# Four heads of the first mixer as one rolling stream

## The chip, the core and the metric

The kernel runs on one core of one Trainium2 chip. The metric is the device time of one execution in microseconds; of several executions the median is given. The engines named below are PE (TensorE, matrix products and transposes), DVE (VectorE), ACT (ScalarE), POOL (GpSimd) and SP (SyncE, whose queue issues all the transfers).

## The reference, cut to what matters

Two layers of a block run one after the other on 1024 latent tokens and 256 context tokens. In each layer a projection feeds three mixers: a gated linear recurrence (HGRN2, the "first mixer", four heads of width 64), an mLSTM and a windowed attention; their outputs are gated, projected back and added to the input. The change is in the first mixer alone:

```python
def gla_chunked(q, k, v, logf, s0):            # chunks of L tokens
    b = jnp.cumsum(logf, axis=2)
    decay = jnp.exp(jnp.where(mask, b[:, :, :, None] - b[:, :, None, :], -jnp.inf))
    A = jnp.einsum('bnthk,bnshk,bntshk->bntsh', q, k, decay)
    o_intra = jnp.einsum('bntsh,bnshv->bnthv', A, v)
    U = jnp.einsum('bnshk,bnshv->bnhkv', k * jnp.exp(bL[:, :, None] - b), v)
    # scan over the chunks: S = exp(bL) * S + U
    o_inter = jnp.einsum('bnthk,bnhkv->bnthv', q * jnp.exp(b), s_prev)
    return (o_intra + o_inter).reshape(B, T, H, dv), s_fin
```

It runs forward and backward over the tokens; the two outputs are added, normed per head and gated.

## The kernel before, in words

**One head.** `hgrn_load` brings a head's arrays from DRAM into three tiles with five transfers: `KQ` (forward key above, query below), `QK` (the other way round) and `FG` (the forget factors of both directions). `hgrn_head` then goes through these steps, each with its line:

- `E = KQ*QK` on DVE (940), its column sums on PE into a PSUM tile `gd`, copied by ACT into the chunk matrices `AT` (944); two DVE products with `FG` (946).
- Six levels (`LEVELS`, the tokens of a chunk of 64 split in halves of 1, 2, 4, ... 32). In each, `gram` makes 40 small products (`gr`, each two PE instructions), DVE copies them under a mask into `AT` (936), and DVE multiplies the decay into `KQ`, `QK` (954) and `FG` (955). The next level's `gr` needs those products.
- The keys are transposed on PE (`ktp`) and copied by ACT into `Kt` (968), in a group of 2 and one of 8 token tiles.
- `up` products on PE; the recurrence over the 20 chunks in both directions on DVE, one small instruction for each chunk and direction (999).
- `op` products on PE: those with `AT` first, those with the states `S` after a pause; ACT copies the result into `O2` (1024). `hgrn_norm` norms two heads at a time and transposes the result (`yAp`).

**Two pairs.** `mixers` runs the heads in two pairs. `lockstep` takes the generators of a pair and always goes on with the one that is due first. Heads 0 and 2 have slots 0, 1, 2 for their three tiles, heads 1 and 3 slots 6, 7, 8 (`wt(6 * i + j, ...)`); the states later take the slot of `KQ` and `Kt` that of `FG`. So the second pair's transfers have to wait until the first pair is through. The second call of `lockstep` holds the norm of the first pair and heads 2 and 3.

**The order of work.** PE's instructions stay in the order in which the program emits them. `drive` makes that order with a clock of its own (`clk`), to which each product adds a planned time:

```python
n = max(n, 256) if rhs.dtype == F32R else 4 * (max(n, out.shape[0]) if small else n)
clk[0] += n / (4800.0 if small else 2400.0)
```

When a generator yields a number, that many microseconds of this clock are filled with products of the next projection unit (`ORDER`: `f` forget factors, `G` gates `ppGz`, `ppGo`, `e`, `c`, `d` the attention's values `ppCv`, keys `ppCk`, queries `ppCq`). `NEED` holds some units back: `e0` until the first pair is normed (`A0`), `c0`, `d0` and `G4` until all four heads are through (`o1`). Instructions of the other engines are placed by a scheduler with priorities; within the stage, copies out of a projection's PSUM tile stand above the mixer's work (`ev`). PSUM tiles come from three pools of two buffers each: `pp` (projections), `pb` (two banks: `gd`, `gr`, the larger `up`), `pm` (one bank: `ktp`, the first `up` group, `op`, `yAp`).

Of the kernel before, what the change touches and what calls it, by code (L numbers as in the profile page):

```python
# [10 lines left out]
F32 = mybir.dt.float32  # L11
# [4 lines left out]
ALU = mybir.AluOpType  # L16
# [3 lines left out]
P = 128  # L20
# [30 lines left out]
SE = 2  # L51
EV = 3500
NEED = {"p2": ("b0",), "p3": ("b1",), "e0": ("A0",), "c0": ("o1",), "d0": ("o1",), "G4": ("o1",), "e1": ("vt0",), "c1": ("s0",), "d1": ("s0",), "e2": ("vt1",), "c2": ("s1",), "d2": ("s1",), "G7": ("s1",), "W": ("c2", "d2", "e2", "G7", "gg")} | {f"o{t}": ("W",) for t in range(10)}
WAIT = {"gate": 28.0, "rot": 14.0, "qkT": 0.8, "ov": 1.4, "yB": 9.0, "load": 8.0, "gr": 4.0, "ktp": 1.5, "up": 8.0, "upc": 3.0, "yA": 9.0, "vtp": 0.5, "sc": 1.2, "sc0": 3.0, "t": 0.3, "pt": 1.2, "W": 8.0, "prep": 8.0, "st": 6.0, "y": 2.0}


def build(tc, I, out, dbg=None, upto="all"):
# [6 lines left out]
def _build(ctx, tc, nc, I, out, dbg, upto):  # L64
# [13 lines left out]
    def wt(i, shape, name, dtype=F32):  # L78
        return wk.tile(shape, dtype, tag=f"s{i}", name=name)
# [793 lines left out]
    def hgrn_f(l, h, hx):  # L873
# [14 lines left out]

        yield from proj_cm(hx, I["wcm"][l, h], ALLG, evac_f, f"Af{nm}")

    def hgrn_load(l, h):
        tok0 = TC if l == 1 else 0
        i = h % 2
        nm = f"{l}_{h}"

        KQ, QK, FG = S["A", h] = [wt(6 * i + j, [P, TA], f"{n_}{nm}") for j, n_ in enumerate(("KQ", "QK", "FG"))]
        f, w = slice(0, 64), slice(64, 128)
        q = qsd[l][h * 64:(h + 1) * 64, tok0:]
        if tok0:
            G.memset(KQ[w, 0:tok0], 0.0)  # L900
            G.memset(QK[f, 0:tok0], 0.0)
        nc.sync.dma_start(KQ[f], fsd[l][0, h, 0:64])
        nc.sync.dma_start(QK[w], fsd[l][0, h, 64:128])
        nc.sync.dma_start(KQ[w, tok0:], q)
        nc.sync.dma_start(QK[f, tok0:], q)
        nc.sync.dma_start(FG, fsd[l][1, h])

    def hgrn_head(l, h):
# [9 lines left out]
        AT = wk.tile([P, NT, LA], F32, tag=f"h{i}", name=f"AT{nm}")
        if i == 0:
            vt = wt((4, 3)[p], [P, NT, P], f"Vt{l}_{p}")  # L920
            nc.sync.dma_start(vt, vsd[l][p])
            S["V", p] = [vt]

        def gram(m, li):

# [10 lines left out]
                V.copy_predicated(v4(AT[:, y0:, :]), v4(lmask[:, li:li + 1, :].to_broadcast([P, NT - y0, LA])), src)  # L936


        E = wt(((9, 12), (9, 10))[p][i], [P, TA], f"E{nm}")
        V.tensor_tensor(E[:, tok0:], KQ[:, tok0:], QK[:, tok0:], op=ALU.mult)  # L940
        ps = pb.tile([P, 1024], F32, tag="pb", name=f"gd{nm}")
        for t in range(y0, NT):
            mm(ps[:, (t - y0) * LA:(t - y0 + 1) * LA], E[:, t * P:(t + 1) * P], ones)
        A.activation(AT[:, y0:, :], ps[:, 0:(NT - y0) * LA].rearrange("p (c t) -> p c t", t=LA), AF.Copy)
        for X, r in ((QK, f), (KQ, w)):
            V.tensor_tensor(X[r, tok0:], X[r, tok0:], FG[r, tok0:], op=ALU.mult)
        yield WAIT["gr"]
# [10 lines left out]
        dec = sm.tile([P, NCH], F32, tag="dec", name=f"dec{nm}")  # L958
        V.tensor_copy(dec, FG[:, ::LA])

        kt = wt(6 * i + 2, [P, NT, P], f"Kt{nm}")
        for t0, n in ((0, 2), (2, 8)):
            pss = [pm.tile([P, 512], F32, tag="pm", name=f"ktp{nm}_{t0}_{d}") for d in range(2)]
            for t in range(n):
                for ps, X, r in zip(pss, (KQ, QK), (f, w)):
                    tr(ps[:, t * LA:(t + 1) * LA], X[r, (t0 + t) * P:(t0 + t + 1) * P], r)
            for ps, r in zip(pss, (f, w)):
                A.activation(kt[:, t0:t0 + n, r], ps[:, 0:n * LA].rearrange("p (t c) -> p t c", c=LA), AF.Copy)
            yield WAIT["ktp"]
# [7 lines left out]
        for t0, n in ((0, 2), (2, 8)):  # L977
            ups = {}
            if not t0:
                while clk[0] < at.get("upc", 0.0):  # L980
                    yield at["upc"] - clk[0]
                at["upc"] = clk[0] + WAIT["upc"]
            if t0:
                ps = pb.tile([P, 1024], F32, tag="pb", name=f"up{nm}_{t0}")
                banks = [ps[:, 0:512], ps[:, 512:1024]]
            else:
                banks = [pm.tile([P, 512], F32, tag="pm", name=f"up{nm}_{t0}_{e}") for e in range(2)]
            for t in range(n):
# [12 lines left out]

        while f"g{h ^ 1}" not in done:
            yield 1.0
        if len(S["V", p]) == 1:
            S["V", p].append(wt((5, 10)[p], [P, NT, P], f"O2{l}_{p}"))
        Vt, O2 = S["V", p]
        for t0, n in ((0, 2), (2, 8)):
            if t0 < y0:
                continue
            ps = pm.tile([P, 512], F32, tag="pm", name=f"op{nm}_{t0}")  # L1010

            for part in range(2):
                if part and t0:
                    yield WAIT["st"]
                for t in range(t0, t0 + n):
                    for e in range(2):
                        c = 2 * t + e
                        es = slice(64 * e, 64 * e + 64)
                        o = ps[es, (t - t0) * 64:(t - t0 + 1) * 64]
                        if part:  # L1020
                            mm(o, QK[:, c * LA:(c + 1) * LA], Sx[:, c, :], False, t == t0 + n - 1)
                        else:
                            mm(o, AT[es, t, :], Vt[es, t, hs], t == t0, False)
            A.activation(O2[:, t0:t0 + n, hs], ps[:, :n * 64].rearrange("p (t v) -> p t v", v=64), AF.Copy)

    def hgrn_norm(l, p):
        y0 = NCX if l == 1 else 0
        tok0 = y0 * P
        O2 = S["V", p][1]
        n = NT - y0  # L1030
        SQ = wt((11, 3)[p], [P, NT, P], f"SQA{l}_{p}")
# [6 lines left out]
        yT = wt((11, 3)[p], [P, TA], f"yTA{l}_{p}")  # L1038
# [386 lines left out]
    for l in range(2):  # L1425
# [5 lines left out]
        def mixers():  # L1431
            yield "p0"
            yield from mlstm_gates(l)
            for h in range(HB):
                yield from flushing(mlstm_head(l, h))
            for p in range(2):
                for u in ("v", f"q{p}", f"f{2 * p}", f"f{2 * p + 1}"):
                    yield u
                if p:
                    hgrn_load(l, 2)  # L1440
                hgrn_load(l, 2 * p + 1)
                if not p:
                    yield WAIT["load"]
                pace[1] = math.inf
                ev[0] = PR + 300
                yield from flushing(lockstep([hgrn_norm(l, 0)] * p + [hgrn_head(l, 2 * p), hgrn_head(l, 2 * p + 1)], 2 + p))
            ev[0] = EV
            done.add("o1")
            pace[:] = 4.0, clk[0]
# [128 lines left out]
```

## Time and profile before

| | |
|---|---|
| median of 3 runs | 2074.26 us (2068.77 to 2077.22) |
| the profiled execution | 2070.56 us |
| its span | 2068.8 us |
| PE busy | 1825.0 us, 88% |
| DVE busy | 1288.3 us, 62% |
| mean granted clock of PE | 0.933 |

The profile shows one execution. "Busy" is the time in which an engine has an instruction under way; matrix products are pipelined, so that a busy PE need not be at its peak. The clock column of a window is the mean of the clock that PE was granted: 1.00 is 2.4 GHz, 0.50 is 1.2 GHz. A releaser is the instruction whose end let a waiting one start.

### The profile page before, as it was taken

The page shows a single profiled execution, that of the slowest core. Times are in us where ns is not written, and L with a number is a line of the kernel's source. Part 1 is how long each engine was busy: PE and PEld are TensorE (multiplying, and loading weights), DVE is VectorE, ACT ScalarE, POOL GpSimd, SP SyncE. Part 2 cuts the span into 40 slices and gives each one's busy share as a digit, 9 for nine tenths or more (in the row PEclk, how much of TensorE's full clock was granted, in tenths as well). Part 3 has the DMA queues.
Part 4 walks back from the last instruction along what each step waited for, and adds up shares of the span by engine and source line. Part 5 has one row for each costly group of instructions (what it writes and reads, how often), then busy time and mean ns, then how long its engine had stood idle before and what let it go on. Part 6 is the DMA issues. An engine that isn't in the chain of part 4 may idle for free.

```text
span 2068.8 us, 38016 instructions
## 1 busy us (share of the span) xinstructions
PE 1825.0 (88%) x14506; PEld 1567.1 (76%) x14506; DVE 1288.3 (62%) x3209; ACT 829.8 (40%) x2003; POOL 558.0 (27%) x574
## 2 busy tenths in 40 slices
PE   6979889988776989999799888999988889999798
PEld 3978778876665767878688888989867667777587
DVE  7597678667676477455465586464577754454554
ACT  5423434342011265566634334253421125454731
POOL 5342352320110211110434454234202120201512
PEclk8989999998797999999999989999998899999799
DMA  7221333441311233233743112142503112223643
GB/s 305 62 81 57 110 115 124 145 139 35 85 51 34 69 124 104 76 101 115 249 145 114 44 52 75 48 126 96 146 32 113 32 62 86 81 79 106 200 139 104
DMA packets 143287, 210.01 MB, mean 102 GB/s; under 512 B 13193, under 2 KB 77737, under 8 KB 143105
## 3 DMA queue, kind: packets, MB, share of 16 engines
q1 hardware_dynamic: 143104, 207.58, 31.3%
q8 instruction: 115, 1.88, 0.4%
q14 instruction: 68, 0.55, 0.1%
HBM read 164.83 MB, written 42.70 MB: 100 GB/s over the span
## 4 chain that ended last, share of the span: by engine, by line
PE 43%; DVE 12%; ACT 6%; issue 3%; DMA 3%; POOL 2%; SPq 0%; DVEq 0%; POOLq 0%; ACTq 0%
PE u L319 9%; PE ppGz L319 5%; PE ppB L319 4%; PE ppCk L319 4%; PE sc L319 3%; PE ppCq L319 3%; PE ppCv L319 2%; PE ppAf L319 2%; PE ppGo L319 2%; DVE S L999 2%; ACT S L1170 1%; PE tw L324 1%; ACT S L1172 1%; DVE dj L199 1%; PE ov L319 1%
## 5 line engine op out<-in xcount | busy, mean ns | idle before, releaser
L319 PE MATMUL ppB<-whB,hh 128*128 128x288 f32 (+3 forms) x640 | 197.7, 309 | 25.8 <-ACT Vx L610 20.0
L319 PE MATMUL ppB<-whB,hl 128*128 128x288 f32 (+3 forms) x640 | 192.2, 300 | 1.0 <-DVE hl L293 1.0
L319 PE MATMUL ppB<-wlB,hh 128*128 128x288 f32 (+3 forms) x640 | 192.3, 301 | 0.0
L319 PE MATMUL u<-ow,yh 128*128 128x512 f32 (+1 forms) x684 | 182.9, 362 | 2.3 <-ACT u L1404 1.8
L319 PE MATMUL ppGz<-hh,whGz 128*128 128x512 f32 (+1 forms) x320 | 134.5, 420 | 25.2 <-DVE cv L1080 14.8
L199 DVE CUSTOM_DVE_ANT_0 dj<-wm,crows 128x256 bf16<-128x256 f32 x256 | 130.9, 511 | 27.7 <-DMA wm<-in_w_mod 24.3
L319 PEld LDWEIGHTS ppB<-whB,hh 128*128 128x128 f32 x640 | 124.5, 195 | 29.1 <-ACT Vx L610 22.5
L319 PEld LDWEIGHTS u<-ow,yh 128*128 128x128 f32 x684 | 124.1, 191 | 24.1 <-ACT u L1404 2.6
L319 PE MATMUL ppGz<-hl,whGz 128*128 128x512 f32 (+1 forms) x320 | 125.8, 393 | 0.0
L319 PE MATMUL ppGz<-hh,wlGz 128*128 128x512 f32 (+1 forms) x320 | 125.4, 392 | 0.0
L319 PEld LDWEIGHTS ppB<-whB,hl 128*128 128x128 f32 x640 | 124.2, 194 | 1.3 <-DVE hl L293 1.3
L319 PEld LDWEIGHTS ppB<-wlB,hh 128*128 128x128 f32 x640 | 124.6, 195 | 0.1
L319 PE MATMUL u<-ow,yl 128*128 128x512 f32 (+1 forms) x324 | 114.7, 372 | 4.8 <-POOL yl L1315 4.8
L319 PEld LDWEIGHTS ppGz<-hh,whGz 128*128 128x128 f32 x320 | 65.3, 204 | 37.1 <-issue 15.4
L329 POOL TENSOR_TENSOR wlGz<-wrGz,whGz 128x512 fp32r<-128x512 f32 x32 | 45.0, 1408 | 174.4 <-PE ppGz L319 45.7
L999 DVE SCALAR_TENSOR_TENSOR S<-S,dec,up 64x64 f32<-64x64 f32 x288 | 80.5, 280 | 9.3
L319 PEld LDWEIGHTS gr<-QK,KQ 64*64 64x64 f32 x1728 | 57.9, 140 | 37.5 <-issue 30.1
L319 PE MATMUL gr<-QK,KQ 64*64 64x32 f32 x1728 | 61.9, 225 | 27.3 <-DVE QK L954 27.2
L1170 ACT ACTIVATE S<-S,nmx 128x544 f32<-128x544 f32 (+1 forms) x96 | 75.0, 783 | 22.9 <-DVE nmx L1168 22.4
L319 PE MATMUL ppAf<-hh,whAf 128*128 128x512 f32 (+1 forms) x192 | 77.6, 404 | 4.8 <-DVE fe L884 4.8
L1283 POOL TENSOR_TENSOR ow<-wro,ow 128x256 fp32r<-128x256 f32 (+1 forms) x44 | 43.4, 1017 | 123.0 <-ACT ow L1282 122.8
L1168 DVE CUSTOM_DVE_ANT_0 S<-sc,bias 128x544 f32<-128x544 f32 (+1 forms) x96 | 70.9, 768 | 8.1 <-PE sc L319 8.0
(464 smaller groups left out, 5394.2 us busy)
## 6 DMA issues: line engine op xcount, KB each, us to landing
wm<-in_w_mod SPq DMA_DIRECT2D x64, 256.0 KB
bias<-in_rpb SPq DMA_DIRECT2D x48, 320.0 KB
bias<-in_rpb SPq DMA_DIRECT2D x48, 272.0 KB
ygr<-gTd SPq DMA_DIRECT2D x36, 256.0 KB
wm<-in_w_first SPq DMA_DIRECT2D x16, 512.0 KB
wrGz<-in_wcm SPq DMA_DIRECT2D x32, 256.0 KB
gTd<-gz SPq DMA_DIRECT2D x32, 256.0 KB
wro<-in_w_out SPq DMA_DIRECT2D x32, 256.0 KB
```

The lines of the kernel that those rows point to most:

```text
L199: V.tensor_tensor_reduce(out=junk, in0=w, in1=r, scale=1.0, scalar=0.0, op0=ALU.mult, op1=ALU.add, accum_out=dst[:, i:i + 1])
L319: return PE.matmul(out, lhsT=lhsT, rhs=rhs, start=start, stop=stop)
L324: return PE.transpose(out, x, ident[r, r])
L329: (eng or G).tensor_tensor(wl, raw, wh.bitcast(F32), op=ALU.subtract)
L999: V.scalar_tensor_tensor(Sx[r, nx, :], Sx[r, c, :], dec[r, c:c + 1], ups[c][r], op0=ALU.mult, op1=ALU.add)
L1168: V.tensor_tensor_reduce(out=S2, in0=ps[i][:, 512 - nk:512 + TC], in1=bias[i][:, :nk + TC] if nk else zero.to_broadcast([P, TC]), scale=-1 ...
L1170: A.activation(S2, S2, AF.Exp, scale=-1.0, bias=nmx[:, o], accum_out=den[:, o])
L1172: A.activation(S2, S2, AF.Copy, scale=den[:, o])
L1283: G.tensor_tensor(w, raw[:, c:c + n], h.bitcast(F32), op=ALU.subtract)
```

## The change

The four heads become one stream: `lockstep([head 0, head 1, head 2, norm of 0 and 1, head 3], 3)` with three places. Head 2 has tiles of its own (slots 9, 12, 10) and is loaded at the start, once its projections are done. It makes `E` and the two `FG` products, and then waits for `x0`, the mark that head 0 is through. Head 3 takes the place of head 1 and its slots; it loads once `x1` is set. `AT`, `gd` and the transfer of `Vt` come after the `FG` products, behind a planned pause `gd` of 4 us. The key transposes go direction by direction, each in a `pm` tile of its own taken in turn; the first `up` group takes a `pb` tile, as the second does. `E`, `Vt`, `O2` and the tiles of the norm change slots.

```diff
+    HSL = ((0, 1, 2), (6, 7, 8), (9, 12, 10), (6, 7, 8))
...
+        if p:
+            while not all(u in done for u in (f"q{p}", f"f{h}")) or i and f"x{h - 2}" not in done:
+                yield 1.0
+            hgrn_load(l, h)
         KQ, QK, FG = S["A", h]
...
+        if p:
+            yield WAIT["load"]
+        E = wt((5, 11, 11, 0)[h], [P, TA], f"E{nm}")
         V.tensor_tensor(E[:, tok0:], KQ[:, tok0:], QK[:, tok0:], op=ALU.mult)
+        for X, r in ((QK, f), (KQ, w)):
+            V.tensor_tensor(X[r, tok0:], X[r, tok0:], FG[r, tok0:], op=ALU.mult)
+        yield WAIT["gd"]
+        while p and f"x{h - 2}" not in done:
+            yield 1.0
+        AT = wk.tile([P, NT, LA], F32, tag=f"h{i}", name=f"AT{nm}")
         ps = pb.tile([P, 1024], F32, tag="pb", name=f"gd{nm}")
...
-        for X, r in ((QK, f), (KQ, w)):
-            V.tensor_tensor(X[r, tok0:], X[r, tok0:], FG[r, tok0:], op=ALU.mult)
-        yield WAIT["gr"]
+        if i == 0:
+            vt = wt((4, 11)[p], [P, NT, P], f"Vt{l}_{p}")
+            nc.sync.dma_start(vt, vsd[l][p])
+            S["V", p] = [vt]
+        yield 1.0
...
         for t0, n in ((0, 2), (2, 8)):
-            pss = [pm.tile([P, 512], F32, tag="pm", name=f"ktp{nm}_{t0}_{d}") for d in range(2)]
-            for t in range(n):
-                for ps, X, r in zip(pss, (KQ, QK), (f, w)):
+            for X, r in ((KQ, f), (QK, w)):
+                ps = pm.tile([P, 512], F32, tag="pm", name=f"ktp{nm}_{t0}_{r.start}")
+                for t in range(n):
                     tr(ps[:, t * LA:(t + 1) * LA], X[r, (t0 + t) * P:(t0 + t + 1) * P], r)
-            for ps, r in zip(pss, (f, w)):
                 A.activation(kt[:, t0:t0 + n, r], ps[:, 0:n * LA].rearrange("p (t c) -> p t c", c=LA), AF.Copy)
             yield WAIT["ktp"]
...
-            if t0:
-                ps = pb.tile([P, 1024], F32, tag="pb", name=f"up{nm}_{t0}")
-                banks = [ps[:, 0:512], ps[:, 512:1024]]
-            else:
-                banks = [pm.tile([P, 512], F32, tag="pm", name=f"up{nm}_{t0}_{e}") for e in range(2)]
+            ps = pb.tile([P, 1024], F32, tag="pb", name=f"up{nm}_{t0}")
+            banks = [ps[:, 0:512], ps[:, 512:1024]]
...
-        while f"g{h ^ 1}" not in done:
-            yield 1.0
...
+        done.add(f"x{h}")
...
-            for p in range(2):
-                for u in ("v", f"q{p}", f"f{2 * p}", f"f{2 * p + 1}"):
-                    yield u
-                if p:
-                    hgrn_load(l, 2)
-                hgrn_load(l, 2 * p + 1)
-                if not p:
-                    yield WAIT["load"]
-                pace[1] = math.inf
-                ev[0] = PR + 300
-                yield from flushing(lockstep([hgrn_norm(l, 0)] * p + [hgrn_head(l, 2 * p), hgrn_head(l, 2 * p + 1)], 2 + p))
+            for u in ("v", "q0", "f0", "f1"):
+                yield u
+            hgrn_load(l, 1)
+            yield WAIT["load"]
+            pace[1] = math.inf
+            ev[0] = PR + 300
+            yield from flushing(lockstep([hgrn_head(l, 0), hgrn_head(l, 1), hgrn_head(l, 2), hgrn_norm(l, 0), hgrn_head(l, 3)], 3))
```

## Rows read from the trace of the kernel before

**Rows 1.** The page, part 1: busy time, share of the span, count, by engine.

```profile
PE 1825.0 (88%) x14506; PEld 1567.1 (76%) x14506; DVE 1288.3 (62%) x3209; ACT 829.8 (40%) x2003; POOL 558.0 (27%) x574
```

**Rows 2.** Windows, first layer: length, busy PE, PEld, DVE, ACT, POOL (count), clock, DMA share, GB/s.

```profile
459.22:497.70 38.48, 32.59 (x1027) 28.11 (x1026) 35.83 (x61) 4.18 (x8) 2.88 (x2) 0.91 0.14 49
497.70:551.99 54.29, 44.35 (x401) 36.05 (x400) 27.12 (x87) 11.02 (x21) 4.32 (x8) 0.81 0.21 63
551.99:573.64 21.65, 13.46 (x56) 12.12 (x55) 11.82 (x8) 2.64 (x4) 11.11 (x5) 0.61 0.42 95
573.64:616.03 42.39, 32.90 (x1035) 28.28 (x1035) 39.81 (x73) 4.18 (x8) 6.49 (x4) 0.92 0.19 62
616.03:680.19 64.16, 45.03 (x402) 36.71 (x401) 31.52 (x118) 10.69 (x22) 3.99 (x7) 0.81 0.09 27
```

**Rows 3.** The same for the second pair of heads in the second layer.

```profile
1575.20:1593.88 18.68, 12.33 (x60) 10.80 (x55) 9.82 (x8) 1.79 (x3) 6.37 (x8) 0.63 0.42 101
1593.88:1634.28 40.40, 33.01 (x859) 28.06 (x858) 36.24 (x58) 5.26 (x9) 9.33 (x6) 0.92 0.15 48
1634.28:1685.20 50.92, 42.53 (x351) 32.73 (x350) 26.01 (x90) 12.12 (x24) 5.72 (x8) 0.87 0.08 27
```

**Rows 4.** Waits from 440 to 700 us: who waited for whom, total, times, longest.

```profile
PE ppGz L319 <- DVE cv L1080: 9.1, 1, 9.1
PE op L319 <- ACT O L1024: 5.9, 2, 5.5
PE ktp L324 <- DVE S L999: 5.2, 2, 3.0
PE ktp L324 <- ACT Kt L968: 4.6, 4, 1.6
```

**Rows 5.** Waits from 1480 to 1700 us.

```profile
PE ppGz L319 <- DVE cv L1080: 5.8, 1, 5.8
PE ktp L324 <- ACT Kt L968: 2.6, 2, 1.3
```

**Rows 6.** Timeline of the SP queue and of VectorE in the first layer's gap.

```profile
552.04 0.44 SPq L902 DMA_DIRECT2D KQ<-fsd  x1
563.18 1.48 DVE L940 TENSOR_TENSOR E<-KQ,QK 128x1280 f32<-128x1280 f32 x1
```

**Rows 7.** Windows of the first pair's level stretch: tile gr alone, then line 954 alone.

```profile
459.22:497.70 38.48, 17.31 (x960) 16.21 (x960) 13.53 (x24) 0.91 0.14 49
459.22:497.70 38.48, 18.35 (x23) 0.91 0.14 49
```

**Rows 8.** Windows of tile ppAf alone, from gd on, first and second layer.

```profile
437.90:703.15 265.25, 0.00 (x0) 0.00 (x0) 0.68 (x1) 1.73 (x3) 0.85 0.21 64
1473.70:1702.03 228.33, 0.00 (x0) 0.00 (x0) 0.68 (x1) 1.71 (x3) 0.88 0.23 71
```

**Rows 9.** Windows of tile gd alone: first and second pair, first layer; second pair, second layer.

```profile
450.30:455.00 4.70, 4.57 (x40) 4.45 (x40) 0.73 (x2) 1.00 0.18 57
551.99:573.64 21.65, 9.06 (x40) 8.68 (x40) 1.41 (x2) 0.61 0.42 95
1575.20:1593.88 18.68, 7.30 (x32) 6.98 (x32) 1.19 (x2) 0.63 0.42 101
```

**Rows 10.** Timeline of PE: key transposes of one head, first layer.

```profile
500.38 0.22 PE L324 MATMUL ktp<-ident,KQ 64*128 64x64 f32 x1
500.38 0.22 PE L324 MATMUL ktp<-ident,QK 64*128 64x64 f32 x1
500.75 0.22 PE L324 MATMUL ktp<-ident,KQ 64*128 64x64 f32 x1
```

**Rows 11.** Windows of VectorE alone, between gd and the first level copies, first layer.

```profile
452.00:460.60 8.60, 0.69 (x1) 1.00 0.43 115
```

**Rows 12.** Windows of line 999 alone, a stretch with nothing between its instructions.

```profile
656.50:666.60 10.10, 8.95 (x32) 1.00 0.07 25
```

**Rows 13.** Windows of tile ppGz alone, after head 3's end, second layer.

```profile
1685.20:1702.03 16.83, 9.94 (x42) 7.82 (x42) 2.07 (x3) 2.58 (x5) 1.00 0.36 125
```

More of the change, by code (lines that the diff above doesn't have):

```diff
@@ L53 @@
 NEED = {"p2": ("b0",), "p3": ("b1",), "e0": ("A0",), "c0": ("o1",), "d0": ("o1",), "G4": ("o1",), "e1": ("vt0",), "c1": ("s0",), "d1": ("s0",), "e2": ("vt1",), "c2": ("s1",), "d2": ("s1",), "G7": ("s1",), "W": ("c2", "d2", "e2", "G7", "gg")} | {f"o{t}": ("W",) for t in range(10)}
-WAIT = {"gate": 28.0, "rot": 14.0, "qkT": 0.8, "ov": 1.4, "yB": 9.0, "load": 8.0, "gr": 4.0, "ktp": 1.5, "up": 8.0, "upc": 3.0, "yA": 9.0, "vtp": 0.5, "sc": 1.2, "sc0": 3.0, "t": 0.3, "pt": 1.2, "W": 8.0, "prep": 8.0, "st": 6.0, "y": 2.0}
+WAIT = {"gate": 28.0, "rot": 14.0, "qkT": 0.8, "ov": 1.4, "yB": 9.0, "load": 8.0, "gr": 4.0, "ktp": 1.5, "up": 8.0, "upc": 3.0, "yA": 9.0, "vtp": 0.5, "sc": 1.2, "sc0": 3.0, "t": 0.3, "pt": 1.2, "W": 8.0, "prep": 8.0, "gd": 4.0, "st": 6.0, "y": 2.0}
 def build(tc, I, out, dbg=None, upto="all"):
@@ L889, in hgrn_f @@
         yield from proj_cm(hx, I["wcm"][l, h], ALLG, evac_f, f"Af{nm}")
+    HSL = ((0, 1, 2), (6, 7, 8), (9, 12, 10), (6, 7, 8))
     def hgrn_load(l, h):
         tok0 = TC if l == 1 else 0
-        i = h % 2
         nm = f"{l}_{h}"
-        KQ, QK, FG = S["A", h] = [wt(6 * i + j, [P, TA], f"{n_}{nm}") for j, n_ in enumerate(("KQ", "QK", "FG"))]
+        KQ, QK, FG = S["A", h] = [wt(HSL[h][j], [P, TA], f"{n_}{nm}") for j, n_ in enumerate(("KQ", "QK", "FG"))]
         f, w = slice(0, 64), slice(64, 128)
@@ L915, in hgrn_head @@
         hs = slice(64 * i, 64 * i + 64)
+        if p:
+            while not all(u in done for u in (f"q{p}", f"f{h}")) or i and f"x{h - 2}" not in done:
+                yield 1.0
+            hgrn_load(l, h)
         KQ, QK, FG = S["A", h]
[L918 to L922, printed above, removed]
         def gram(m, li):
@@ L936, in gram @@
                 V.copy_predicated(v4(AT[:, y0:, :]), v4(lmask[:, li:li + 1, :].to_broadcast([P, NT - y0, LA])), src)
-        E = wt(((9, 12), (9, 10))[p][i], [P, TA], f"E{nm}")
+        if p:
+            yield WAIT["load"]
+        E = wt((5, 11, 11, 0)[h], [P, TA], f"E{nm}")
         V.tensor_tensor(E[:, tok0:], KQ[:, tok0:], QK[:, tok0:], op=ALU.mult)
+        for X, r in ((QK, f), (KQ, w)):
[4 more added lines that the diff above has]
+        AT = wk.tile([P, NT, LA], F32, tag=f"h{i}", name=f"AT{nm}")
         ps = pb.tile([P, 1024], F32, tag="pb", name=f"gd{nm}")
@@ L959, in hgrn_head @@
         V.tensor_copy(dec, FG[:, ::LA])
-        kt = wt(6 * i + 2, [P, NT, P], f"Kt{nm}")
+        kt = wt(HSL[h][2], [P, NT, P], f"Kt{nm}")
         for t0, n in ((0, 2), (2, 8)):
-            pss = [pm.tile([P, 512], F32, tag="pm", name=f"ktp{nm}_{t0}_{d}") for d in range(2)]
-            for t in range(n):
-                for ps, X, r in zip(pss, (KQ, QK), (f, w)):
+            for X, r in ((KQ, f), (QK, w)):
+                ps = pm.tile([P, 512], F32, tag="pm", name=f"ktp{nm}_{t0}_{r.start}")
+                for t in range(n):
                     tr(ps[:, t * LA:(t + 1) * LA], X[r, (t0 + t) * P:(t0 + t + 1) * P], r)
-            for ps, r in zip(pss, (f, w)):
                 A.activation(kt[:, t0:t0 + n, r], ps[:, 0:n * LA].rearrange("p (t c) -> p t c", c=LA), AF.Copy)
@@ L970, in hgrn_head @@
         A.activation(QK[w, tok0:], KQ[w, tok0:], AF.Copy)
-        Sx = wt(6 * i, [P, NCH, LA], f"S{nm}")
+        Sx = wt(HSL[h][0], [P, NCH, LA], f"S{nm}")
         G.memset(Sx[f, 0, :], 0.0)
@@ L1000, in hgrn_head @@
             yield WAIT["up"] if t0 else WAIT["upc"]
-        while f"g{h ^ 1}" not in done:
-            yield 1.0
         if len(S["V", p]) == 1:
-            S["V", p].append(wt((5, 10)[p], [P, NT, P], f"O2{l}_{p}"))
+            S["V", p].append(wt((5, 1)[p], [P, NT, P], f"O2{l}_{p}"))
         Vt, O2 = S["V", p]
@@ L1024, in hgrn_head @@
             A.activation(O2[:, t0:t0 + n, hs], ps[:, :n * 64].rearrange("p (t v) -> p t v", v=64), AF.Copy)
+        done.add(f"x{h}")
     def hgrn_norm(l, p):
+        while any(f"x{2 * p + i}" not in done for i in range(2)):
+            yield 1.0
         y0 = NCX if l == 1 else 0
@@ L1030, in hgrn_norm @@
         n = NT - y0
-        SQ = wt((11, 3)[p], [P, NT, P], f"SQA{l}_{p}")
+        SQ = wt(3, [P, NT, P], f"SQA{l}_{p}")
         G.tensor_tensor(SQ[:, y0:], O2[:, y0:], O2[:, y0:], op=ALU.mult)
@@ L1037, in hgrn_norm @@
         V.tensor_tensor(O2v, O2v, r[:, :, None].to_broadcast([P, 2 * n, 64]), op=ALU.mult)
-        yT = wt((11, 3)[p], [P, TA], f"yTA{l}_{p}")
+        yT = wt(3, [P, TA], f"yTA{l}_{p}")
         yield WAIT["yA"]
```

## The prediction

> **What bounds the kernel now.** I read the page's first part, then windows over the stage of the first mixer in both layers, then the waits in it, then the timelines of its gap. The page shows PE busy 88% of the span [rows 1]: outside the stage only PE work itself could be shortened, and the change shortens none. So the question is how much PE idle time, or time at a low clock, the stage holds and what ends it.
>
> The windows cut the stage by what PE does: levels of the first pair, its transposes, `up` and `op`, then the gap from the last `op` to the first `gr` of the second pair, then the second pair [rows 2, 3]. In the first layer PE is idle 38.48 - 32.59 = 5.9, 9.9, 8.2, 9.5 and 19.1 us in the five stretches. In the second layer the gap, levels and rest of the second pair hold 6.4, 7.4 and 8.4 us. The gaps also have the lowest clock, 0.61 and 0.63. In the levels DVE is the fuller engine: 35.83 of 38.48 us.
>
> The waits name what PE stands for outside the levels [rows 4, 5]: key transposes for ACT's copies and for the recurrence (5.2 + 4.6 and 2.6 us; both hold `pm` tiles), a gate product for an attention value copy on DVE (9.1 and 5.8 us, DVE being in the recurrence), `op` for ACT (5.9 us). In the gap SP issues head 3's first transfer only at 552.04, when the first pair is done, and `E` of that head begins at 563.18 [rows 6]; `gd`, next in PE's fixed order, stands behind it with everything that follows.
>
> One head alone: a level has a gram of 17.31/12 = 1.44 us on PE and 35.83/12 = 2.99 us on DVE [rows 2, 7], of which the copies are 13.53/12 = 1.13 and line 954 is 18.35/23 x 2 = 1.60. These follow one another: 4.4 us. The planner sets 4 us of other products between two grams of one head, so 1.44 + 4.0 = 5.4 us: with one head in its levels PE waits for nothing. With two, 38.48/6 = 6.4 us for both, and DVE decides.
>
> **The change part by part.** Reference is the profiled execution, 2070.56 us (span 2068.8); the median of the runs, 2074.26, is 3.7 above it.
>
> *Head 2 loaded early.* It polls for `q1` and `f2`; no forget product runs in either layer from `gd` on [rows 8], so the load goes out at the stage's start, five transfers where the DMA share of the following levels is 0.14 [rows 2]. That moves its loads ahead of the level stretch in SP's queue, and `Vt` behind `gd`; the count of transfers stays. At `x0` head 2 needs only `gd` and its grams, beside projection products. The gap's idle goes: 8.2 + 6.4 = 14.6 us. Its low clock goes in part: `gd` costs 9.06 us there for 40 instructions, 4.57 us in the first pair of the first layer, and 7.30 us for 32 in the second layer, which at the first pair's price is 3.66 [rows 9]: 4.5 + 3.6 us. Together 22.7; I take 20, because head 3's `gd` still comes in the middle of things. Lower end 8, the first layer's idle alone.
>
> *Head 3 loaded after `x1`.* On the planner's clock it comes 8 (load) + 4 (`gd`) + 1 us after head 1. From transfer to `E` took 563.18 - 552.04 = 11.1 us, so PE, with 13 us of other products in front, should not wait. Head 2 has 13/5.4 = 2.4 levels done by then; some three levels run as a pair, the rest of head 3's alone at PE's pace. The second pair's levels hold 9.5 + 7.4 = 16.9 us of PE idle; I take back half, 8 (0 to 17).
>
> *Key transposes and first `up` group.* A `pm` tile each in turn, and `up` in `pb`: the waits for `pm`, 5.2 + 4.6 + 2.6 = 12.4 us, lose their cause except for ACT's copies themselves. I take 6 (0 to 12).
>
> *Order of the transposes.* Today those on `KQ` and `QK` start together, and seven of each take 500.75 - 500.38 = 0.37 us for six steps, 0.062 a step [rows 10]. If only the pairing gives that, eight and two steps for each direction in turn add 10 x 0.062 = 0.62 us for a head, 5 us for eight heads; if not, nothing. I take 2, as ACT now copies the one while PE transposes the other. The Trainium skill (TensorEngine Tiling (Array Packing), Tiling Modes, Key Properties) says that different tiles of the array run weight loads and products in parallel, which speaks against this edit. By that rule the 5 us stand whole and the sum below is 3 us worse; the row agrees that the two halves overlap, and does not show one half alone.
>
> *`E` and the `FG` products of head 2 among the levels of the first pair.* Three DVE operations; `E` takes 1.48 us [rows 6], the other two have as many columns: 4.5 us, and 4/5 of it, 3.6, in the second layer with 1024 columns instead of 1280. The DVE has room just before, 0.69 us busy of 8.60 [rows 11], but the planner places them after the first grams. Loss 6 us (0 to 8). Behind them wait the level copies, and the next gram for those.
>
> *Recurrence of head 2 within head 3's levels.* A new wait. The 30 instructions after the second `up` group take 10.10/32 = 0.316 us each [rows 12], 9.5 us. If DVE does them in one run, a level of head 3 stands behind it, and PE's next gram, with all projection products after it, waits 9.5 - 4 = 5.5 us a layer. Loss 11 us (0 to 30, see the slow rival).
>
> *Recurrences apart instead of together.* The copies that held PE up, 9.1 + 5.9 + 5.8 = 20.8 us [rows 4, 5], stood behind two heads' recurrences at once, 60 instructions or 19 us; now behind one at a time. I take back half, 10 (0 to 21).
>
> *Projection products.* Head 3's 13 us of pauses and the single levels ask for more of them inside the stage: the 13 less what head 2's grams fill (2.4 x 1.44), about 9.5 us, a little more at the pair's end. The second layer has only 9.94 us of gate products left after head 3 [rows 13]; units behind `o1` can't come earlier. Once they are used up PE runs on the heads alone. Loss 3 us (0 to 5).
>
> *Nothing:* the marks and the lockstep of three cost no instruction. `O2` of the second pair lies in slot 1, which the attention's first transposed values take next; PE's `yAp` transposes stand right before these in its order, so the slot is free by then. If that cover went, the copy would wait for the one transpose group ahead of it, under a microsecond. `E` in 5, 11 and 0 and `Vt` in 11 take slots whose last readers are PE instructions well ahead.
>
> **Sum:** 20 + 8 + 6 + 10 = 44 us back, 2 + 6 + 11 + 3 = 22 us lost: 22 us. 2070.56 - 22 = 2048.6; with 3.7 us for the median, **2052 us**. It assumes that idle taken from PE in the stage shortens the whole: the gate products not used there come after it, among attention work whose PE share is that of the kernel or higher.
>
> **The rivals.**
> *No change.* The end of the stage is set by head 3, whose load still waits for head 1, and which has 13 us of pauses more than the pair had. Head 2's head start then only moves projection products forward, and the low clock, the level idle and the copies stay as they are. What is left is the gap's idle, 14.6, less 6, 11 and 3: -5, so 2070.56 + 5 + 3.7 = 2079 us; without the new wait 2069. For it speaks that head 3's chain of levels is as long as before; against it, that single levels are PE's, not DVE's.
>
> *Slower: the recurrence holds `pb`.* One mechanism: head 2's second `up` group keeps one of the two `pb` tiles until its recurrence ends, and head 3's grams, one `pb` tile each, run into it; PE stands still in its fixed order. In the first layer the recurrences were drawn out by other DVE work (the rest of the second pair, 64 us, has only 31.52 us of DVE [rows 2]), so a tile can be held far longer than 9.5 us. Without this term the sum is 33 us gained; it decides from 33/2 = 16.5 us a layer, and is visibly slower from 22. At 25 us a layer the time is 2070.56 - 33 + 50 + 3.7 = 2091 us. Against it: with one head in levels a single `pb` tile is enough, because the next gram waits for DVE anyway.
>
> *Much faster.* All waits named go and nothing new comes: 22.7 + 16.9 + 12.4 + 20.8 = 72.8, less 8 and 5: 60 us, so 2014 us.
>
> *The early load isn't early*, because SP's queue stands at that time behind a transfer that waits. Then the gap moves but stays: 20 us less gained, 2072 us. It belongs with no change.
>
> **How the numbers follow.** A run of this kernel can be told from no change at about 0.5%, 10.4 us: below 2063.9 is faster, above 2084.6 slower. The forecast, with its own range of 2040 to 2066 (none of the new wait, or some half of the gains with unknown ends gone), has 0.55; much faster 0.11; no change with the late load 0.20; the slow rival 0.14. A little of the no-change case falls on either side: faster 0.66, same 0.20, slower 0.14. The range is 2024 to 2088: it leaves out most of the much faster case and the worse part of the slow one.
>
> **What would show it.** Right: between head 0's last `op` and head 2's first `gr` some 4 us instead of 21.65 and 18.68 to the second pair's; `E` of head 2 at the first pair's start; the clock there above 0.9; single grams with 18 projection instructions between them; waits of `ktp` nearly gone. Wrong: a wait of `gr` for line 999 longer than 6 us, or of `gd` of head 3 for its `E`; the first pair's levels longer than 44 us; a second layer in which PE has no projection product left before head 3 is through. The prediction is wrong above all if these new waits, or a later end of head 3, cost as much as the gaps held.

## The result, and the profile after

The changed kernel takes 2034.53 us in the median (2030.47 to 2039.9) against 2073.58 for the kernel before on the same chip: a ratio of 0.9817, 95% interval 0.9801 to 0.9833. That is 39 us less where 22 were forecast: direction right and inside the stated range of 2024 to 2088, but 1.8 times the size, and below the 2040 to 2066 that the forecast gave its own main case. The profiled execution spans 2031.0 us, 37.8 less than before.

The page, part 1, of the changed kernel, answers to [rows 1]. PE's instructions are the same in number, and take 18.1 us less.

```profile
PE 1806.9 (89%) x14506; PEld 1552.8 (76%) x14506; DVE 1298.8 (64%) x3209; ACT 829.2 (41%) x2003; POOL 559.1 (28%) x574
```

Windows over the whole stage, from the last forget product to the first attention query product, in both layers; first the kernel before, then the changed one (columns as in [rows 2]).

```profile
437.84:717.63 279.79, 220.33 (x3182) 184.13 (x3182) 177.59 (x417) 51.77 (x107) 46.15 (x37) 0.85 0.21 64
1473.63:1714.96 241.33, 206.74 (x2666) 168.19 (x2666) 152.47 (x329) 52.61 (x101) 46.63 (x46) 0.89 0.22 68
```

```profile
431.32:690.16 258.84, 213.12 (x3182) 180.08 (x3182) 178.06 (x388) 50.51 (x103) 45.86 (x39) 0.88 0.21 65
1449.47:1676.09 226.62, 198.36 (x2667) 161.56 (x2667) 154.79 (x333) 52.89 (x103) 47.71 (x43) 0.93 0.22 69
```

PE does the same instructions in both, give or take one. The two stages together went from 521.1 to 485.5 us, and these 35.6 us are nearly all of the gain. PE idle (length less busy) fell from 94.1 to 74.0 us, by 20. PE busy fell from 427.1 to 411.5, by 15.6: the same products at a higher granted clock. A second profile of the changed kernel (e9, below) has 77.0 us of idle and 408.1 us of PE busy in its two stages.

Windows of the changed kernel's first layer, in the order of [rows 2]: levels of the first pair; its transposes, `up` and `op`; the rest, in two parts, to the last `op` of head 3. The last row is the second layer's second stretch.

```profile
460.79:500.57 39.78, 33.56 (x1029) 29.51 (x1030) 39.20 (x63) 4.48 (x9) 1.50 (x1) 0.87 0.08 26
500.57:541.49 40.92, 37.83 (x415) 31.74 (x418) 26.50 (x87) 11.23 (x22) 4.03 (x7) 1.00 0.15 50
541.49:599.02 57.53, 42.53 (x831) 36.35 (x831) 43.33 (x63) 6.97 (x12) 16.91 (x9) 0.76 0.25 73
599.02:662.66 63.64, 56.26 (x696) 46.79 (x695) 39.29 (x123) 12.29 (x25) 8.31 (x10) 0.95 0.10 34
...
1514.87:1554.50 39.63, 39.09 (x425) 31.33 (x425) 26.32 (x86) 11.65 (x22) 9.32 (x12) 1.00 0.18 60
```

The second stretch took 54.29 us and now takes 40.92, at a clock of 1.00 instead of 0.81. The gap is gone as a stretch. The third row is left at a low clock, 0.76.

PE's waits in the changed kernel, stage of the first layer, then of the second.

```profile
PE gr L319 <- DVE QK L965: 12.2, 10, 2.9
PE ppGz L319 <- DVE fe L884: 9.1, 1, 9.1
PE yAp L324 <- DVE O L1045: 8.9, 1, 8.9
PE ppGz L319 <- DVE cv L1088: 6.5, 1, 6.5
...
PE ktp L324 <- ACT Kt L978: 1.2, 3, 0.7
...
PE op L319 <- ACT O L1029: 0.4, 1, 0.4
...
PE gr L319 <- DVE S L1006: 0.2, 1, 0.2
```

```profile
PE gr L319 <- DVE QK L965: 14.6, 8, 6.2
PE ppGz L319 <- DVE fe L884: 4.2, 2, 3.2
PE op L319 <- ACT Kt L978: 3.1, 1, 3.1
```

Against [rows 4, 5] the waits of `ktp` for the recurrence are gone, that of `op` for ACT is 0.4, that of the gate product for `cv` 6.5 once. The wait charged with 11 us, `gr` for the recurrence (now line 1006), is 0.2. New are 9.1 us for `fe` (3.1 before) and 8.9 us of the norm's transposes, `yAp`, for the norm's product.

### The profile page after: what moved, and what is told of

Same layout as the page of the kernel before. It is cut to its first block, busy times and chain, and to the rows that moved or that the text cites. A ratio compares the mean times of both kernels' runs of the same rounds, so it can differ in the third digit from the quotient of the medians.

```text
span 2031.0 us, 37975 instructions
## 1 busy us (share of the span) xinstructions
PE 1806.9 (89%) x14506; PEld 1552.8 (76%) x14506; DVE 1298.8 (64%) x3209; ACT 829.2 (41%) x2003; POOL 559.1 (28%) x574
## 4 chain that ended last, share of the span: by engine, by line
PE 54%; DVE 22%; ACT 7%; issue 5%; DMA 4%; POOL 4%; SPq 0%; DVEq 0%; POOLq 0%; ACTq 0%
PE u L319 9%; PE ppB L319 7%; PE ppGz L319 6%; PE ppCk L319 4%; DVE dj L199 4%; PE ppCq L319 3%; PE sc L319 3%; PE ppAf L319 3%; PE ppCv L319 2%; PE ppAq L319 2%; PE ppGo L319 2%; PE ppAv L319 2%; DVE AT L936 2%; DVE S L1006 2%; ACT S L1178 2%
## 5 line engine op out<-in xcount | busy, mean ns | idle before, releaser
L199 DVE CUSTOM_DVE_ANT_0 dj<-wm,crows 128x256 bf16<-128x256 f32 x256 | 135.9, 531 | 20.7 <-DMA wm<-in_w_mod 17.3
```

Of the source, the lines that this page charges most:

```text
L199: V.tensor_tensor_reduce(out=junk, in0=w, in1=r, scale=1.0, scalar=0.0, op0=ALU.mult, op1=ALU.add, accum_out=dst[:, i:i + 1])
```

## The experiments

The edits are shown against the kernel before, or against the changed one where that is said.

### The buffers alone

**e1_buffers_alone**: the kernel before, with key transposes direction by direction and the first `up` group in `pb`. **e6_up_in_pb_alone**: the second hunk alone.

```diff
-            pss = [pm.tile([P, 512], F32, tag="pm", name=f"ktp{nm}_{t0}_{d}") for d in range(2)]
-            for t in range(n):
-                for ps, X, r in zip(pss, (KQ, QK), (f, w)):
+            for X, r in ((KQ, f), (QK, w)):
+                ps = pm.tile([P, 512], F32, tag="pm", name=f"ktp{nm}_{t0}_{r.start}")
+                for t in range(n):
...
-            for ps, r in zip(pss, (f, w)):
...
-            if t0:
-                ps = pb.tile([P, 1024], F32, tag="pb", name=f"up{nm}_{t0}")
-                banks = [ps[:, 0:512], ps[:, 512:1024]]
-            else:
-                banks = [pm.tile([P, 512], F32, tag="pm", name=f"up{nm}_{t0}_{e}") for e in range(2)]
+            ps = pb.tile([P, 1024], F32, tag="pb", name=f"up{nm}_{t0}")
+            banks = [ps[:, 0:512], ps[:, 512:1024]]
```

> The kernel before with the buffers alone changed: key transposes direction by direction in a pm tile each, first up group in pb; the two pairs stay. Theory A (the head start of head 2 and the filled gap are the bulk, the buffers some 6 us as the prediction has it): ratio to before 0.995 to 0.999, and the first layer's stretch from the first pair's last gr to its last op shrinks from 54.3 us by at most 5. Theory B (the buffers are worth a third or more of the 39 us): ratio 0.990 or less, and that stretch near 41 us, as in the changed kernel.

> The kernel before with only the first up group moved from two pm tiles to pb. If the buffers' gain comes from the pm tiles that the first up group holds until the recurrence has read them (second head's key transposes waiting 5.2 us in the first layer, and what stands behind them), this has most of it: ratio 0.988 to 0.994. If the order of the key transposes is what gains (each direction's copy beside the other's transposes), this has little: 0.996 to 1.000.

Measured: e1 2052.28 us, 0.9898 (0.9857 to 0.9938); e6 2053.52 us, 0.9898 (0.9863 to 0.9932). So this edit is worth some 1.0%, 21 us (the intervals allow 13 to 30), where the prediction took 6; and as far as these intervals tell, all of it comes from `up` leaving `pm`, since e6 has no other edit. The order of the transposes costs and gives nothing that can be measured here. In e1 the stretch from the first pair's key transposes to its last `op` was 49.63 us where the kernel before had 54.29 and the changed kernel 40.92: in the full change something more acts on it. That rest is mostly clock, since idle is 4.9 us in e1 and 3.1 in the changed kernel, PE busy 44.7 and 37.8.

Windows of e6, the four stretches after the first pair's levels, as in [rows 2], and its waits of `ktp` in the first layer.

```profile
497.50:546.00 48.50, 41.53 (x401) 33.78 (x400) 27.13 (x87) 11.02 (x21) 4.31 (x8) 0.89 0.23 70
546.00:568.20 22.20, 13.90 (x57) 12.43 (x55) 11.82 (x8) 2.63 (x4) 11.13 (x5) 0.62 0.41 94
568.20:610.20 42.00, 34.52 (x1031) 29.81 (x1031) 39.97 (x71) 4.18 (x8) 6.49 (x4) 0.84 0.20 62
610.20:668.60 58.40, 43.90 (x406) 35.82 (x404) 31.12 (x121) 10.70 (x22) 3.98 (x7) 0.85 0.10 30
```

```profile
PE ktp L324 <- ACT Kt L968: 4.6, 4, 1.6
```

The wait for the recurrence (5.2 us) is gone, that for ACT's copies stays at 4.6. The first pair's last stretch lost 5.8 us with the same 401 PE instructions: 3.0 of idle (9.94 to 6.97) and 2.8 of PE busy (44.35 to 41.53), at a clock of 0.89 instead of 0.81. The second pair, from its first gram to its last `op`, lost 6.2 (106.55 to 100.40). Half of what the first stretch gained stands in no row of waits. This split is not the same in every execution: in e1 the stretch lost 5.0 us of idle and nothing of PE busy (44.71 us, clock 0.83).

**e2_old_buffers_pair1**: the changed kernel, heads 0 and 1 with the old buffers.

```diff
+            if p == 0:
+                pss = [pm.tile([P, 512], F32, tag="pm", name=f"ktp{nm}_{t0}_{d}") for d in range(2)]
...
+            else:
+                for X, r in ((KQ, f), (QK, w)):
...
+            if t0 or p:
                 ps = pb.tile([P, 1024], F32, tag="pb", name=f"up{nm}_{t0}")
```

> The changed kernel with heads 0 and 1 alone back on the old buffers (both directions' key transposes at once, first up group in two pm tiles); heads 2 and 3 keep the new ones, which they need when they overlap. Theory A: ratio to before 0.982 to 0.985, at most 6 us slower than the changed kernel. Theory B: 12 to 16 us slower than the changed kernel, ratio 0.987 to 0.990, with the stretch from the first pair's last gr to its last op in the first layer back at some 54 us.

Measured: 2042.76 us, 0.9836 (0.9805 to 0.9866); the changed kernel has 0.9817. Inside the rolling stream the buffers of the first pair are worth a few us at most, and the intervals overlap. The first layer's stretch from transposes to last `op` took 45.28 us, 4.4 more than in the changed kernel, not the 54 of theory B. Old buffers for heads 2 and 3 in the stream weren't tried: two `pm` tiles held there would stand in PE's fixed order in front of other heads' transposes.

### The gap without an early load

**e3_pause_only**: the kernel before, where the second pair too yields for the load's planned time. Nothing is loaded earlier; the planner puts projection products in front of `gd`.

```diff
                 hgrn_load(l, 2 * p + 1)
-                if not p:
-                    yield WAIT["load"]
+                yield WAIT["load"]
```

> The kernel before, with the planned pause of 8 us after the loads also ahead of the second pair; nothing is loaded earlier. If the gap costs because PE's order has nothing to do in it (theory C: filling is all, the head start gains nothing of its own), this gains what the gap held, 14 to 20 us: ratio 0.990 to 0.993. If the head start is what gains (theory A), the pause only moves products into the gap while the second pair starts no earlier, and the ratio is 0.995 to 1.000.

Measured: 2044.27 us, 0.984 (0.9816 to 0.9865): 1.6% from one line, 33 us, more than the theories expected. Windows of e3, the gap in both layers, which answer to the third row of [rows 2] and the first of [rows 3]:

```profile
552.71:574.54 21.83, 19.77 (x136) 17.47 (x133) 14.07 (x10) 4.38 (x7) 15.14 (x8) 0.92 0.56 131
1562.40:1578.66 16.26, 16.26 (x88) 13.54 (x87) 11.86 (x10) 3.49 (x7) 9.02 (x9) 1.00 0.52 128
```

The gap is as long as before in the first layer (21.83 against 21.65), but PE fills it: 136 instructions instead of 56, idle 2.1 us instead of 8.2, clock 0.92 instead of 0.61. In the second layer idle goes from 6.4 to nothing and the clock from 0.63 to 1.00. The transfers are no earlier: `E` of the second pair begins at 558.81 (557.21 before), and what PE still waits for it is the 2.1 us. The gaps' 12.5 us of idle are not the whole. Over both stages idle fell from 94.1 to 74.0 and PE busy from 427.1 to 415.5; the gate product's waits for `cv` (9.1 and 5.8 us before) are gone as well, while `op` now waits 12.5 us for ACT instead of 5.9.

**e5_pause_and_buffers**, and again in five rounds as **e10_pause_buffers_5_rounds**: e3 and e1 together, without rolling and without an early load. **e9_changed_again**: the changed kernel, five rounds on that same chip.

The edits are those two, shown above.

> The kernel before with the pause ahead of the second pair and the new buffers, no early load and no rolling: the two parts that gained 1.6% and 1.0% alone. Theory C (filling the gap and the buffers are the whole gain; loading head 2 ahead and rolling add nothing): ratio 0.974 to 0.983, as fast as the changed kernel or faster. Theory A' (the head start of head 2 still gives a part): the two overlap, ratio 0.984 to 0.988, slower than the changed kernel by 5 us or more.

> Pause and buffers on the kernel before, no early load and no rolling, now beside the changed kernel in five rounds. Theory C (rolling and the early load add nothing): no slower than the changed kernel, ratio 0.974 to 0.982. Theory A' (they add a part): slower, 0.984 or more.

> The changed kernel itself, beside the next three on the same chip: ratio 0.980 to 0.984 by every theory.

Measured: e5 2025.37 us, 0.9768 (0.9726 to 0.981); e10 2028.56 us, 0.9788 (0.9765 to 0.981); e9 2036.7 us, 0.9842 (0.9816 to 0.9868). On one chip the pause and the buffers beat the changed kernel by 8 us, with intervals that don't meet. The gains add up nearly: 1.6% and 1.0% apart, 2.1 to 2.3% together. So the rolling stream and the early load, together and as built here, are no gain over the pause and the buffers; they cost some 0.4 to 0.5%. Early load and rolling were not run apart from each other.

Windows over the two stages of e5, which has e10's code (for e10 see below):

```profile
436.43:687.52 251.09, 209.94 (x3183) 176.70 (x3182) 172.14 (x395) 50.49 (x103) 43.90 (x37) 0.90 0.23 70
1447.43:1664.83 217.40, 196.11 (x2668) 159.23 (x2666) 151.54 (x329) 52.23 (x101) 46.87 (x46) 0.95 0.25 75
```

Idle in the two stages is 62.4 us in e5 and 60.8 in e10, against 74.0 and 77.0 in the two profiles of the changed kernel: the stream's loss is idle. PE busy tells less: 406.1 in e5 and 415.2 in e10, 9.1 us apart with the same code and work.

The stream does win one wait. The largest that pause and buffers leave, from the waits of e10 in the first layer, is 0.4 us in the changed kernel:

```profile
PE op L319 <- ACT O L1020: 13.2, 2, 12.8
```

### What the rolling stream costs

Timelines of the changed kernel, first layer: VectorE, then ScalarE and PE, ahead of the first pair.

```profile
432.83 2.57 DVE L944 TENSOR_TENSOR QK<-QK,FG 64x1280 f32<-64x1280 f32 x1
435.41 1.49 DVE L944 TENSOR_TENSOR KQ<-KQ,FG 64x1280 f32<-64x1280 f32 x1
...
437.67 1.48 DVE L942 TENSOR_TENSOR E<-KQ,QK 128x1280 f32<-128x1280 f32 x1
...
439.42 1.47 DVE L944 TENSOR_TENSOR QK<-QK,FG 64x1280 f32<-64x1280 f32 x1
440.90 1.49 DVE L944 TENSOR_TENSOR KQ<-KQ,FG 64x1280 f32<-64x1280 f32 x1
...
442.50 0.68 DVE L884 SCALAR_TENSOR_TENSOR fe<-fe,ppAf 128x512 f32<-128x512 f32 x1
```

```profile
439.46 0.28 ACT L838 ACTIVATE nu<-H 128x96 f32<-128x96 f32 x1 [5.96 <-DVE H L836]
...
443.24 0.80 PE L319 MATMUL ppGz<-hh,whGz 128*128 128x512 f32 x1 [9.08 <-DVE fe L884]
```

The program now has the `FG` products of heads 0 and 1 before `gd`. On DVE all four run between the end of the last forget product (431.32) and the last forget gate's `fe`, which frees the tile that a gate product needs. In the kernel before, head 0's pair ran at 426.03, ahead of that end (437.84), and head 1's at 443.68, behind `fe`. Part of the delay goes by way of ACT, which makes the input of `fe` and stands 5.96 us behind a DVE result of the mLSTM. PE waits 9.1 us there; e10 and e3, with the program's old order, wait 3.8 and 4.8. The prediction saw that the `FG` products move among the first pair's levels for head 2, and costed nothing for heads 0 and 1. No run moved them alone, so this cause is read from the order, not shown by an edit.

Windows of the changed kernel around the wait of `yAp`:

```profile
549.00:562.00 13.00, 4.10 (x72) 3.19 (x65) 12.28 (x11) 1.26 (x2) 7.25 (x4) 0.83 0.22 66
562.00:575.00 13.00, 13.00 (x142) 11.18 (x141) 3.11 (x6) 2.28 (x4) 0.00 (x0) 0.52 0.13 52
```

The norm of the first pair is planned between heads, and its product (560.17) comes on DVE behind `E`, both `FG` products of head 3 and a level. PE's fixed order holds `yAp` in front, so PE does 4.1 us of work in 13. Then it has work without a pause for 13 us, at a clock of 0.52: the wait is paid a second time.

**e7_norm_later**: the changed kernel, with that order moved.

```diff
-        yield WAIT["yA"]
+        yield 20.0 if p == 0 else WAIT["yA"]
```

> The changed kernel with a planned pause of 20 us instead of 9 between the norm of the first pair and its transposes. In the changed kernel PE stands 8.9 us in the first layer at these transposes, waiting for the normed output, and 6.2 us in the second just ahead of them. If these are pauses planned too short, the ratio is 0.973 to 0.979, 5 to 15 us faster than the changed kernel; if the wait only moves on (the grams behind then wait for DVE), 0.980 to 0.984.

Measured: 2030.74 us, 0.9789 (0.9757 to 0.9821). The wait of `yAp` for the norm's product is gone, the first layer's stage is 254.85 us instead of 258.84; but `gr` now waits 16.8 us there instead of 12.2. By ratio it is better by 0.3%, inside the intervals.

**e4_E_after_x0**: the changed kernel, with `E` and the `FG` products of head 2 held until head 0 is through (head 3 waits for head 1 in any case, before its load).

```diff
+        while p and f"x{h - 2}" not in done:
+            yield 1.0
         E = wt((5, 11, 11, 0)[h], [P, TA], f"E{nm}")
```

> The changed kernel with head 2 still loaded early, but its E and FG products only after head 0 is through. The prediction charged 6 us for these three DVE operations among the first pair's levels. If that holds, the first pair's levels shorten by some 4 us in the first and 3 in the second layer, and what is lost at head 2's start (4.5 us of DVE and the 4 us pause ahead of its gd, with other products in it) is less: ratio 0.977 to 0.982, that is 0 to 8 us faster than the changed kernel. If their place is worth it, 3 to 10 us slower: 0.983 to 0.987.

Windows of e4, levels of the first pair, first and second layer; in the changed kernel 39.78 and 38.74.

```profile
466.44:503.91 37.47, 29.66 (x1019) 26.35 (x1018) 36.95 (x58) 4.33 (x8) 1.50 (x1) 0.91 0.06 21
1475.58:1511.36 35.78, 30.88 (x830) 25.75 (x829) 34.14 (x58) 3.50 (x6) 2.80 (x2) 0.90 0.11 34
```

The levels are 2.3 and 3.0 us shorter: 5.3, against the 6 of the prediction. The whole, 2035.86 us and 0.9801 (0.9777 to 0.9824), is not told apart from the changed kernel. Its stage is 254.88 us in the first layer, 4.0 shorter, and 231.77 in the second, 5.2 longer; what was lost there was not followed up.

**e8_head3_in_head0_slots**: the changed kernel, with head 3 loaded after head 0 instead of head 1, into head 0's tiles, and the norm of heads 0 and 1 taken into the stream after head 3. **e12_roll_and_norm**: e8 with the edit of e7.

```diff
-    HSL = ((0, 1, 2), (6, 7, 8), (9, 12, 10), (6, 7, 8))
+    HSL = ((0, 1, 2), (6, 7, 8), (9, 12, 10), (0, 1, 2))
...
-            while not all(u in done for u in (f"q{p}", f"f{h}")) or i and f"x{h - 2}" not in done:
+            while not all(u in done for u in (f"q{p}", f"f{h}")) or i and "x0" not in done:
...
-        E = wt((5, 11, 11, 0)[h], [P, TA], f"E{nm}")
+        E = wt((5, 11, 11, 8)[h], [P, TA], f"E{nm}")
...
-            S["V", p].append(wt((5, 1)[p], [P, NT, P], f"O2{l}_{p}"))
+            S["V", p].append(wt((5, 10)[p], [P, NT, P], f"O2{l}_{p}"))
...
-            yield from flushing(lockstep([hgrn_head(l, 0), hgrn_head(l, 1), hgrn_head(l, 2), hgrn_norm(l, 0), hgrn_head(l, 3)], 3))
+            yield from flushing(lockstep([hgrn_head(l, 0), hgrn_head(l, 1), hgrn_head(l, 2), hgrn_head(l, 3), hgrn_norm(l, 0)], 3))
```

> The changed kernel with head 3 in the slots of head 0 and taken into the stream when head 0 is through, so that its load starts 5 us earlier and its pauses run before head 1 ends; the norm comes after it. If head 3's late start sets the end of the stage (the rival 'no change' of the prediction, which held that its 13 us of pauses eat the head start), this gains 4 to 10 us over the changed kernel: ratio 0.975 to 0.979. If the stage is filled with projection products anyway, the same as the changed kernel: 0.980 to 0.983.

> The changed kernel with both of the edits that gained over it one by one: head 3 in the slots of head 0, and the norm's transposes 20 planned us after the norm. If the two gains (some 9 and 5 us) have different causes they add: ratio 0.972 to 0.976. If both only fill the same gap: 0.976 to 0.979.

Measured: e8 2027.68 us, 0.977 (0.9743 to 0.9797); e12 2027.53 us, 0.9789 (0.9766 to 0.9812). Both are some 0.5% faster than the changed kernel, by intervals that don't meet: e8 against its first measurement (0.9817, on another chip), e12 against e9 on the same chip. That fits a cost of head 3's late load, as the rival of no change had it though not in its size; but e8 also moves the norm, and the two were not run apart. The edit of e7 adds nothing on top. Built this way the stream is level with pause and buffers: 2027.53 us against 2028.56 on one chip.

### The best version

**e11_pause_buffers_norm**: e10 with the one line of e7.

> The same with the norm's transposes of the first pair 20 instead of 9 planned us after the norm. In the pairs the norm's transposes stand between two planned grams, with a wait of ACT of some 2.5 us in the first layer: if such waits are all that is left of short pauses, 0 to 5 us faster than without, ratio 0.973 to 0.979; if the delay takes e0 out of reach, slower, 0.980.

Windows over the whole stage, e10, then e11:

```profile
441.55:697.49 255.94, 216.31 (x3183) 181.95 (x3182) 170.77 (x392) 50.04 (x101) 44.08 (x37) 0.87 0.22 67
1454.89:1674.91 220.02, 198.89 (x2666) 162.02 (x2666) 151.55 (x329) 52.37 (x101) 47.57 (x46) 0.94 0.24 74
```

```profile
438.98:687.17 248.19, 207.92 (x3183) 174.90 (x3182) 171.96 (x395) 50.45 (x103) 43.65 (x37) 0.91 0.23 70
1446.54:1663.06 216.52, 195.98 (x2667) 159.96 (x2666) 152.46 (x329) 52.10 (x101) 47.94 (x46) 0.94 0.25 75
```

Measured: 2020.06 us, 0.9754 (0.9727 to 0.9781), 52 us less than the kernel before and 17 less than the changed one on that chip; its interval overlaps e10's a little, and e5's by more. Against e10's profile the first layer's stage is 7.8 us shorter: PE busy fell by 8.4, at a clock of 0.91 instead of 0.87, and idle rose from 39.6 to 40.3. That step is clock, and it is not shown to come from the edit: e5, with e10's code, has a stage of 251.09 us at 0.90, and its profiled execution (2019.24 us) is as fast as e11's (2020.06). Whether the line gains anything over e10 stays open.

## Why the prediction was right in sign and short in size

**What bounds it** held: the gain lies in the two stages, 35.6 of 37.8 us. What failed is how it was counted. The prediction priced the low clock in the gap alone, 4.5 and 3.6 us; elsewhere a wait counted by its length. PE busy at equal work gave 15.6 and 19.0 us in the two profiles of the changed kernel, 11.9 and 21.0 in those of pause and buffers (e10, e5), and 23.2 in e11. Idle fell by 20.1 us, near the net of 22 that was forecast for idle and the gap's clock, but that is luck: as the next paragraphs show, the terms were off in both directions, and two waits stood in none of them.

**Recurrence of head 2 within head 3's levels, 11 us charged: 0.2 measured.** The step that failed most. The changed kernel's windows of tile `gr` alone, from where head 2's recurrence begins (611.2):

```profile
610.00:625.00 15.00, 1.37 (x80) 1.29 (x80) 0.89 (x2) 0.91 0.16 54
625.00:640.00 15.00, 0.00 (x0) 0.00 (x0) 0.00 (x0) 0.86 0.03 10
```

A level has 80 of these instructions (960/12 in [rows 7]): one gram of head 3 was left, and it waited 0.2 us. The lead of 2.4 levels was nearly right: three grams of head 2 ran before head 3's first. What the prediction left out is the time between head 2's last gram and its recurrence, 15.8 us here (595.40 to 611.21), filled with its transposes and first `up` products; head 3 made two of its last three grams in it. DVE in the same stretch:

```profile
611.21 8.39 DVE L1006 SCALAR_TENSOR_TENSOR S<-S,dec,up 64x64 f32<-64x64 f32 x27
619.53 0.89 DVE L936 COPY_PREDICATED AT<-lmask,gr 128x320 f32<-128x320 uint8 x2
```

The copy of head 3's last gram (done at 614.57) did stand behind the recurrence, as forecast, but it was the last level, so no gram waited for it. PE waited in the first layer for the `cv` copy instead, 6.5 us. The slower rival, a `pb` tile held by the recurrence, showed no such wait.

**Key transposes and first `up` group, 6 us taken: about 21 alone** (e1, e6). The place was right, a `pm` tile held through the recurrence; the size was off, because the named wait is not its whole price: both stages together lost 19.3 us of idle in e1 and 11.9 in e6, where 5.2 stood in the row of that wait. Beside the other parts of the change the edit is worth less: some 0.5 to 0.7% on top of the pause (e3 against e10 and e5), a few us for the first pair in the stream (e2). Why the second pair gained 6.2 us in e6 is only argued: the same tiles, the same wait.

**Order of the transposes, 2 us: nothing measurable** (e1 equals e6). The row: the group of sixteen in the changed kernel ran from 503.06 to 504.07, 1.01 us, against 0.72 before (500.26 to 500.98), both at a clock of 1.00. The Trainium skill (TensorEngine Tiling (Array Packing), Tiling Modes, Key Properties) says that different tiles of the array work in parallel; the trace agrees in direction, with 0.29 us a group, and the whole did not lose by it.

**Head 2 loaded early, 20 us taken.** The sign that was named came: timeline of PE in the changed kernel, head 0's last `op`, then `gd`, then the first `gr` of head 2.

```profile
535.45 1.15 PE L319 MATMUL op<-S,QK 128*64 128x64 f32 x32
536.53 2.45 PE L319 MATMUL gd<-ones,E 128*128 128x64 f32 x20
...
541.42 0.24 PE L319 MATMUL gr<-QK,KQ 64*64 64x32 f32 x1
```

That is 4.8 us from `op`'s end to `gr`, where some 4 were forecast, with PE busy throughout at a clock of 1.00; in the second layer it is 3.3 us. The load was early: `E` of head 2 ran at 460.90, at the start of the first pair's levels, so the rival of an early load that isn't early did not come. (One reading was off: the two `FG` transfers of the second pair went out from 519.69 on in the kernel before, and 552.04 was the first of head 3's other four. No term rests on it.) But the reason was wrong: e3 fills the same gap with the transfers where they were, and gains 33 us. What the gap lacked was work in PE's fixed order, not an early transfer.

**Recurrences apart, 10 us:** the copies that held PE up fell from 20.8 to 6.5 + 0.4 us, so 13.9. The term is not isolated: in e3, where the recurrences stay together, the same waits fell to 12.5 us. **`E` and `FG` among the levels, 6 us lost:** 5.3 in the levels, but nothing in the whole (e4). **Second pair's levels, 8 us,** can't be read by itself, since pairs and single heads now overlap. **Projection products, 3 us lost:** no run tried it; the second layer's stage had a mean clock of 0.93 and 28.3 us idle, 6.3 less than before.

**Not in the sum at all:** the moved `FG` products of heads 0 and 1 (6.0 us more wait for `fe`), and the norm between the heads (8.9 us and a low clock behind it). They are the largest named part of what the stream gives back against e10. Not settled: the rest of that difference; what each wait costs in clock behind it; and a shift of some us ahead of the stage from kernel to kernel (the stage began between 431 and 442 us), which limits what differences of a few us can say.

## What to carry to other kernels

Where an engine works in an order fixed beforehand and idles behind a transfer, first plan the transfer's time into that order, so that other work is put in front: here one line gave 1.6%, nearly what the whole restructured stream with its new buffers gave (1.8%). A tile held through a slow chain of another engine blocks whatever shares its pool, and moving its one user to another pool gave 1.0%. Count a stretch by idle and by clock: about half of the stages' gain in the changed kernel was the same instructions, run faster. Take the clock part from more than one profile, since it differed by 9.1 us between two executions of one kernel, where idle differed by 1.7.

## What the runs showed of the hardware that had not been expected

The low clock came with a wait and lasted beyond it: after 8.9 us of idle, 142 PE instructions took all of 13 us at a granted clock of 0.52, close to the lower of the two levels, and after the 9.1 us of waiting for `fe` the next 13.05 us of unbroken work had a clock of 0.81, while in the stretch from 500.57 to 541.49, with 3.1 us of idle in 40.9, the clock was 1.00. Of the changed kernel's gain 15.6 us, of e11's 23.2, were PE busy time at equal instruction counts; two profiles of one kernel differed by up to 9.1 us in it (e10 and e5).
